# One step of a hybrid decoder layer on one core: fewer transposes in the mixer, other buffers and scales for the sample states

## The chip, the core and the metric

The kernel runs on 1 of the 8 cores of one Trainium2 chip. The time is the device time of one execution in microseconds; the table below gives the median of three runs. The core has a matrix engine (TensorE, PE in the profile; PEld is its weight load), VectorE (DVE), ScalarE (ACT), GpSimd (POOL), and a queue of transfers issued by SyncE (SP).

## The reference

One layer of width 2048 is applied to 16 learned meta tokens, 256 prompt tokens and 8 sample tokens, each sample with its own recurrent states. It is FFN, mixer, FFN, each with a residual and a layer norm.

```python
x <- LN1(alpha*x + 0.5*SwiGLU_1(x))
x <- LN2(alpha*x + Mixer(x))      # retention and HGRN2 side by side, gated, one output projection
x <- LN3(alpha*x + 0.5*SwiGLU_2(x))

# a chunk of retention (8 heads of 256), per-head decay gamma
o     = (q k^T * D) v + (q * decay) S
S_new = gamma^C S + (k * decay)^T v
# HGRN2 (16 heads of 128): the same with a forget gate f per channel and k = 1 - f
```

The prompt starts from a zero state; each sample takes one step (C = 1) from its given state, so its new state is `gamma S + k v` (retention) or `f S + k v` (HGRN2) and its output is q times that. Outputs are y for prompt and samples and the four sets of new states.

## The kernel before

Everything is held as features by tokens: 128 partitions of features, 280 columns of tokens (16 meta, 256 prompt, 8 samples). Every weight matrix is streamed once from memory in units of eight 128x128 blocks (`stream`, `raw`, three buffers). ScalarE rounds a unit to a high part (`whi`, line 187), VectorE computes the rest (`wlo`, line 188), and TensorE makes three products for each block (`dense`, line 217): high weights with the high and the low part of x, low weights with the high part.

The mixer works by u = 0 to 7: one retention head of 256 (two column blocks c = 0, 1) and two HGRN heads of 128 (h = 0, 1). `project` runs the dense projections of u (f, q_h, i_h, q_r, k_r, v_r) and the gates of u - 1. Two generators, `mix_hg(u)` and `mix_ret(u)`, do the rest of the mixer in pieces: `pump` is called after each step of a projection and lets a generator go on when the steps that it yielded are over. TensorE's instructions run in just this program order (`manual_schedule` for PE); for the other engines and SP's queue a scheduler sets the order by priority, and each engine then keeps to it.

`mix_ret(u)`, lines 978 to 1115:
- loads the first four samples' states (`load(0)`, line 988, tile `smr`; its four buffers are shared with the split keys and values `ks`, `vs`), and transposes v and k to tokens by features in blocks of 128, 128 and 24 columns (lines 998 and 1007). The last block has the last 16 prompt tokens and the 8 samples. `ks2` and `vs2` hold its high, high, low and high, low, high parts on three groups of partitions;
- writes the samples' v out to memory (`vrow`, line 720), and reads it back spread over all partitions (`spread`, line 1038, `vbr`, four samples at a time, one buffer);
- computes scores times the decay table into `scr`, in place of `dt` (line 239), and the new prompt state in two halves (line 1049), each copied to `sro` and sent out (lines 1051, 1052). `sro` has one buffer (row d9);
- `gam`, also a tile named `sro`, is set to the head's decay by POOL (line 1062). For both halves e of the samples and both c, ScalarE scales the state by `gam` (line 1067), VectorE adds k v sample by sample (line 1070), and the state goes out (line 1073); after the first half the second `spread` is issued;
- 15 or more steps later the sample products `pqr` (line 1084) multiply `qdr`, which holds each sample's q alone in its own column, with these states; the prompt's outputs follow (`por`), and the samples' rows are transposed into their columns by `sample_columns` (line 729).

`mix_hg(u)`, lines 733 to 968: doubling levels s = 1 to 64 scale K and Q by products of f in `Ts`; at levels 16 and 32 the states of the two heads are loaded (`smh`, `vbh`); then the two blocks of K and its 16 meta columns are transposed for each head (line 900), the meta part split into `km` on three groups of partitions; the sample states are scaled by f (line 906, scale from `fk`) and updated (line 907); `pq` (line 933) multiplies `qdh` with them, head h in columns h * 128 on; `sample_columns` transposes them for each head.

Of the kernel before, what the change touches and what calls it, by code (L numbers as in the profile page):

```python
# [10 lines left out]
F32 = mybir.dt.float32  # L11
# [39 lines left out]

SCORES = ((0, 0, SEQ, P), (SEQ, P - NMETA, 2 * P - P + NMETA, P), (2 * SEQ - P + NMETA, SEQ - NMETA, NMETA, LP - 2 * P))
# [75 lines left out]
def trunk(ctx: ExitStack, tc: tile.TileContext, A, O):  # L128
# [417 lines left out]
    with tc.tile_pool(name="yp", bufs=1) as yp:  # L546
# [7 lines left out]
        with tc.tile_pool(name="mp", bufs=1) as mp:  # L554
# [33 lines left out]
            qdh = tmp("qdh", (P, 2, NS * 32))  # L588
            qdr = tmp("qdr", (P, 2, NS * 32))
# [11 lines left out]
            sc2 = tmp("sc2", (P, NMETA), dt=F32R)  # L601
            for z in (km, vm, ks2, vs2, sc2):
                z = z if len(z.shape) == 2 else z.rearrange("p c f -> p (c f)")
                nc.scalar.copy(z, qdh[:, 0, : z.shape[1]])
# [106 lines left out]
            def upper_upper_lower(out, x):  # L711
# [3 lines left out]
                sub(out[64 : 64 + n], x, out[:n].bitcast(F32))  # L715
# [11 lines left out]
            def sample_columns(on, po, os):  # L727

                nc.tensor.transpose(po[:, 3 * P :], os, ident)
                nc.vector.tensor_copy(  # L730
                    on[:, SEQ:].rearrange("p (e j) -> p e j", e=2), po[:, 3 * P :].rearrange("p (j c) -> p c j", c=32)[:, 0:2, :])

            def mix_hg(u, f, k, q, v):
# [121 lines left out]
                for s in (4, 8):  # L855
                    scale_k(s)
                scale_q(8)
# [35 lines left out]
                on_h[u] = on  # L893
                kts = []
                for h in range(2):
# [6 lines left out]
                    upper_upper_lower(km[:, h, :], pt[:NMETA, 2 * P : 3 * P])  # L902

                    vb, sm = vbs[h], sms[h]
                    for b in range(NS):
                        nc.scalar.activation(sm[:, b, :], sm[:, b, :], AF.Copy, scale=fk[:, 0, h, b : b + 1])
# [30 lines left out]
                nc.scalar.copy(os, pq[:, : 2 * P])  # L937
                yield 4

                def outputs(h):  # L940
# [5 lines left out]
                    sample_columns(on[:, h, :], po, os[:, h * P : (h + 1) * P])  # L946
# [31 lines left out]
            def mix_ret(u, q, k, v):  # L978
# [15 lines left out]
                nc.sync.dma_start(dt, A["dtab"][u])  # L994
                for c in range(2):
                    pt = mx_bank("pt")
                    for b, (t0, n) in enumerate(BLOCKS):
                        nc.tensor.transpose(pt[:n, b * P : (b + 1) * P], v[:, c, t0 : t0 + n], ident)
                    nc.scalar.copy(vt[:, :, c, :], pt[:, : 2 * P].rearrange("p (b f) -> p b f", b=2))
                    nc.scalar.copy(vt2[:NB, c, :], pt[:NB, 2 * P : 3 * P])  # L1000
                    f = slice(c * P, (c + 1) * P)
                    split(vs[:, 0, :, f], vs[:, 1, :, f], vt[:, :, c, :])
                    upper_lower_upper(vs2[:, c, :], vt2[:NB, c, :])
                    yield 1
                    pt = mx_bank("pt")
                    for b, (t0, n) in enumerate(BLOCKS):
                        nc.tensor.transpose(pt[:n, b * P : (b + 1) * P], k[:, c, t0 : t0 + n], ident)
# [242 lines left out]
```

## Time and profile before

| what | us |
|---|---|
| median of 3 runs | 2607.2 (2603.62 to 2609.99) |
| the profiled execution | 2608.29 |
| its span, first to last instruction | 2606.2 |
| TensorE busy in it | 2580.9 |
| VectorE busy | 1703.7 |
| ScalarE busy | 1375.4 |
| POOL busy | 13.7 |

A row of a timeline has the start in us from the span's beginning, the length, the engine, the line of the kernel, the operation, the tile written and the tiles read, the shape, and how many instructions are merged; in brackets stands the engine's idle time before it, and what ended it. A row of waits has who waited for whom, then us in total, times, and the longest. In the grouped rows of the page, the busy us and the mean ns of one stand behind the first bar, and the engine's idle time behind the second. The ends of matmuls are modelled, since they are pipelined: the cost of one is better read from start to start.

### The profile page before, as it was taken

What the parts mean: (1) busy time and instruction counts of PE and PEld (TensorE: products, weight loads), DVE (VectorE), ACT (ScalarE), POOL (GpSimd) and SP (SyncE); (2) the same over time, 40 slices, a digit from 0 to 9 for tenths busy, and PEclk for the clock granted to TensorE, in tenths of its full rate; (3) what the DMA queues carried; (4) which work ended last, traced back from release to release, by engine and by line L of the source; (5) the groups of instructions that cost most, each with busy time, mean ns of one, the idle gap of its engine ahead of it and who ended that gap; (6) DMA issues with size and microseconds to landing.
All of it is one profiled execution on the core that took longest, in us unless ns stands there. A gap on an engine that the chain in (4) does not pass through costs nothing.

```text
span 2606.2 us, 56106 instructions
## 1 busy us (share of the span) xinstructions
PE 2580.9 (99%) x23400; PEld 2546.5 (98%) x23400; DVE 1703.7 (65%) x2859; ACT 1375.4 (53%) x2160; POOL 13.7 (1%) x62
## 2 busy tenths in 40 slices
PE   9999999999999989999999999999999999999999
PEld 9999999999999889999999999999999999999998
DVE  6444454565579777777777777776995555556555
ACT  5444444444456566666666666665564444444444
POOL 0000000000000000000000000000000000000000
PEclk9999999999999999999999999999999999999999
DMA  7555555555566675767676767676656666666664
GB/s 240 184 183 185 186 185 182 184 186 185 182 200 223 216 269 183 265 207 260 210 258 210 256 206 263 203 235 194 193 187 201 195 195 195 195 197 193 197 197 147
DMA packets 154591, 536.25 MB, mean 206 GB/s; under 512 B 17696, under 2 KB 25696, under 8 KB 154336
## 3 DMA queue, kind: packets, MB, share of 16 engines
q1 hardware_dynamic: 154048, 532.37, 63.0%
q8 instruction: 183, 3.00, 0.5%
q14 instruction: 72, 0.59, 0.1%
q10 hardware_dynamic: 288, 0.29, 0.0%
HBM read 501.99 MB, written 30.61 MB: 204 GB/s over the span
## 4 chain that ended last, share of the span: by engine, by line
PE 92%; DVE 4%; DMA 2%; ACT 1%; issue 1%; SPq 0%; POOL 0%; ACTq 0%; POOLq 0%; DVEq 0%
PE up L217 35%; PE dn L217 18%; PE pj_f L217 4%; PE pj_q_h L217 3%; PE wo L217 3%; PE pj_k_r L217 3%; PE pj_v_r L217 3%; PE pj_g_r L217 3%; PE pj_i_h L217 3%; PE pj_q_r L217 3%; PE pj_a_r L217 3%; PE pj_g_h L217 3%; PE pj_a_h L217 3%; DVE wlo L188 2%; DMA vbr<-vrd 1%; PE pqr L1084 1%
## 5 line engine op out<-in xcount | busy, mean ns | idle before, releaser
L188 DVE TENSOR_TENSOR wlo<-raw,whi 128x1024 fp32r<-128x1024 f32 (+1 forms) x869 | 1062.4, 1223 | 748.6 <-ACT whi L187 745.4
L187 ACT CAST whi<-raw 128x1024 fp32r<-128x1024 f32 (+1 forms) x870 | 905.3, 1042 | 911.4 <-PE up L217 413.1
L217 PE MATMUL up<-xh,wlo 128*128 128x280 f32 (+1 forms) x2624 | 726.0, 280 | 1.3 <-DVE wlo L188 1.3
L217 PE MATMUL up<-xh,whi 128*128 128x280 f32 (+1 forms) x2624 | 725.7, 280 | 1.0 <-ACT whi L187 1.0
L217 PE MATMUL up<-xl,whi 128*128 128x280 f32 (+1 forms) x2624 | 725.4, 279 | 0.0
L217 PEld LDWEIGHTS up<-xh,wlo 128*128 128x128 f32 x2624 | 492.5, 189 | 2.3 <-DVE wlo L188 2.3
L217 PEld LDWEIGHTS up<-xh,whi 128*128 128x128 f32 x2624 | 492.6, 189 | 1.3 <-ACT whi L187 1.2
L217 PEld LDWEIGHTS up<-xl,whi 128*128 128x128 f32 x2624 | 492.6, 189 | 0.0
L217 PE MATMUL dn<-hh,whi 128*128 128x280 f32 (+1 forms) x1376 | 384.7, 280 | 0.0
L217 PE MATMUL dn<-hh,wlo 128*128 128x280 f32 (+1 forms) x1376 | 384.3, 279 | 0.0
L217 PE MATMUL dn<-hl,whi 128*128 128x280 f32 (+1 forms) x1376 | 384.3, 279 | 0.0
L217 PEld LDWEIGHTS dn<-hh,whi 128*128 128x128 f32 x1376 | 260.1, 189 | 0.1
L217 PEld LDWEIGHTS dn<-hl,whi 128*128 128x128 f32 x1376 | 260.1, 189 | 0.1
L217 PEld LDWEIGHTS dn<-hh,wlo 128*128 128x128 f32 x1376 | 260.1, 189 | 0.0
L217 PE MATMUL pj_g_r<-xh,whi 128*128 128x264 f32 x256 | 76.8, 300 | 0.0
L217 PE MATMUL pj_g_h<-xh,whi 128*128 128x264 f32 x256 | 73.7, 288 | 0.0
L217 PE MATMUL pj_k_r<-xh,whi 128*128 128x280 f32 x256 | 73.7, 288 | 0.0
L217 PE MATMUL pj_v_r<-xh,whi 128*128 128x280 f32 x256 | 73.5, 287 | 0.0
L217 PE MATMUL pj_v_r<-xh,wlo 128*128 128x280 f32 x256 | 72.4, 283 | 0.3 <-DVE wlo L188 0.3
L217 PE MATMUL pj_k_r<-xh,wlo 128*128 128x280 f32 x256 | 72.5, 283 | 0.0
L217 PE MATMUL pj_k_r<-xl,whi 128*128 128x280 f32 x256 | 72.3, 283 | 0.0
L217 PE MATMUL pj_v_r<-xl,whi 128*128 128x280 f32 x256 | 72.3, 283 | 0.0
(393 smaller groups left out, 5235.6 us busy)
## 6 DMA issues: line engine op xcount, KB each, us to landing
raw<-in_w_up SPq DMA_DIRECT2D x343, 512.0 KB, 4.2
raw<-in_w_in SPq DMA_DIRECT2D x320, 512.0 KB, 4.5
raw<-in_w_dn SPq DMA_DIRECT2D x172, 512.0 KB, 3.4
smr<-in_sr SPq DMA_DIRECT2D x32, 512.0 KB, 4.7
out_srs<-smr SPq DMA_DIRECT2D x32, 512.0 KB, 4.7
raw<-in_w_out SPq DMA_DIRECT2D x32, 512.0 KB, 3.5
smh<-in_sg SPq DMA_DIRECT2D x16, 512.0 KB, 4.7
vbr<-vrd SPq DMA_DIRECT2D x16, 512.0 KB, 4.1
```

What stands on the lines that cost most here:

```text
L187: nc.scalar.copy(hi[:, j:jn, :], raw[:, j:jn, :])
L188: nc.vector.tensor_tensor(out=lo[:, j0:j1, :], in0=raw[:, j0:j1, :], in1=hi[:, j0:j1, :].bitcast(F32), op=ALU.subtract)
L217: nc.tensor.matmul(o, w, t, start=start, stop=stop)
L1084: nc.tensor.matmul(pq[32 * j : 32 * j + 32, :256], qdr[:, c, 32 * b : 32 * b + 32], sms[2 * e + c][:, j, :], start=e + c == 0, stop=e + c ...
```

## The change

- Retention, transposes: only the two blocks of 128 of v and k are transposed for each c. POOL copies the 24 last columns of k and v for both c into `tails` (four groups of 32 columns), which is transposed once, at c = 0. `dec2` is the decay for the last block on two groups of partitions.
- HGRN, transposes: POOL copies K's 16 meta columns of both heads into `meta`, transposed once, with head 0.
- HGRN, samples: `qdh` now puts the q of head h and half e in column 2h + e, so the products of both heads add up in the same 128 columns of `pq`; `osh` has half the width, and one transpose serves both heads. `qdr` gets the same layout, with the same columns as before.
- HGRN, scales: the scaling of the states reads `fs`, a POOL copy of the samples' f that takes the buffer of `T64`, a product of the last doubling level.
- Retention, states: `sro` has two buffers (d9 and a new row, d16). The first half's scale is `gam`, a POOL instruction on `scr` that is clamped to the decay; only the second half's is a memset of an `sro` tile. `vbr` has two samples to a transfer, on two buffers; the first two are issued together, and each further one when the four updates that read an older one are issued. Both scalings of a half come ahead of its updates, and both outgoing transfers behind them.

```diff
-                "sro": "d9",
+                "sro": ["d9", "d16"],
-            qdh = tmp("qdh", (P, 2, NS * 32))
+            qdh = tmp("qdh", (P, 4, ALONE))
+            qdh_at = [qdh.rearrange("p a c -> p (a c)")[:, 256 * h :] for h in range(2)]
+            qdr_at = [qdr.rearrange("p a c -> p (a c)")[:, 2 * ALONE * c :] for c in range(2)]
...
             def alone(qd, q):
-                for e in range(2):
-                    nc.vector.tensor_copy(qd[:, :, 128 * e + e : 128 * e + 128 : 32], q[:, :, SEQ + 4 * e : SEQ + 4 * e + 4])
+                nc.vector.tensor_copy(
+                    qd[:, :, : 128 : 32].rearrange("p (c e) j -> p c e j", e=2),
+                    q[:, :, SEQ:].rearrange("p c (e j) -> p c e j", e=2))
...
@@ mix_hg @@
+                nc.gpsimd.tensor_copy(meta[:, :, :NMETA], K[:, :, :NMETA])
...
+                fs = tmp("fs", (P, 2, NS), tag="T64")
+                nc.gpsimd.tensor_copy(fs, fk[:, 0])
...
-                    for b, (t0, n) in enumerate(((NMETA, P), (NMETA + P, P), (0, NMETA))):
-                        nc.tensor.transpose(pt[:n, b * P : (b + 1) * P], K[:, h, t0 : t0 + n], ident)
+                    for b in range(2):
+                        t0 = NMETA + b * P
+                        nc.tensor.transpose(pt[:, b * P : (b + 1) * P], K[:, h, t0 : t0 + P], ident)
+                    x = pt[:64, 2 * P : 3 * P]
+                    if h == 0:
+                        nc.tensor.transpose(x, meta.rearrange("p h t -> p (h t)"), ident)
+                        for i in range(2):
+                            upper_upper_lower(km[:, i, :], x[32 * i : 32 * i + NMETA], 32 * i)
...
-                        nc.scalar.activation(sm[:, b, :], sm[:, b, :], AF.Copy, scale=fk[:, 0, h, b : b + 1])
+                        nc.scalar.activation(sm[:, b, :], sm[:, b, :], AF.Copy, scale=fs[:, h, b : b + 1])
...
-                            pq[j : j + 32, h * P : (h + 1) * P], qdh[:, h, 32 * b : 32 * b + 32], sms[h][:, b, :],
-                            start=b < 4, stop=b >= 4, tile_position=(0, j))
-                os = tmp("osh", (P, 2 * P))
+                            pq[j : j + 32, :P], qdh_at[h][:, 32 * b : 32 * b + 32], sms[h][:, b, :],
+                            start=h == 0 and b < 4, stop=h == 1 and b >= 4, tile_position=(0, j))
+                os = tmp("osh", (P, P))
...
-                    sample_columns(on[:, h, :], po, os[:, h * P : (h + 1) * P])
+                    if h == 0:
+                        sample_columns(on, po, os)
...
@@ mix_ret @@
+                for i, x in enumerate((k, v)):
+                    nc.gpsimd.tensor_copy(tails[:, 2 * i : 2 * i + 2, :NB], x[:, :, 2 * P :])
                 for c in range(2):
                     pt = mx_bank("pt")
-                    for b, (t0, n) in enumerate(BLOCKS):
-                        nc.tensor.transpose(pt[:n, b * P : (b + 1) * P], v[:, c, t0 : t0 + n], ident)
+                    for b in range(2):
+                        nc.tensor.transpose(pt[:, b * P : (b + 1) * P], v[:, c, b * P : (b + 1) * P], ident)
...
-                    for b, (t0, n) in enumerate(BLOCKS):
-                        nc.tensor.transpose(pt[:n, b * P : (b + 1) * P], k[:, c, t0 : t0 + n], ident)
+                    for b in range(2):
+                        nc.tensor.transpose(pt[:, b * P : (b + 1) * P], k[:, c, b * P : (b + 1) * P], ident)
+                    if c == 0:
+                        nc.tensor.transpose(pt[:, 2 * P : 3 * P], tails.rearrange("p i t -> p (i t)"), ident)
...
+                gams = [tmp("gam", (P, 1))]
+                nc.gpsimd.tensor_scalar(
+                    out=gams[0], in0=scr[:, 0:1], scalar1=GAMMA[u], scalar2=GAMMA[u], op0=ALU.min, op1=ALU.max)
...
-                def spread(e):
-                    vbs.append(tmp("vbr", (P, 4, 256)))
-                    nc.sync.dma_start(vbs[e], vrow[4 * e : 4 * e + 4, :].partition_broadcast(P))
+                def spread(i):
+                    if i < 4:
+                        vbs.append(tmp("vbr", (P, 2, 256), bufs=2))
+                        nc.sync.dma_start(vbs[i], vrow[2 * i : 2 * i + 2, :].partition_broadcast(P))
 
                 spread(0)
+                spread(1)
...
-                gam = tmp("sro", (P, 1))
-                nc.gpsimd.memset(gam, GAMMA[u])
+                gams.append(tmp("sro", (P, 1)))
+                nc.gpsimd.memset(gams[1], GAMMA[u])
                 for e in range(2):
-                    vb = vbs[e]
+                    ss = sms[2 * e : 2 * e + 2]
+                    for sm in ss:
+                        nc.scalar.activation(sm, sm, AF.Copy, scale=gams[e])
+                    for i in (2 * e, 2 * e + 1):
+                        for c in range(2):
+                            for b in (2 * i, 2 * i + 1):
+                                x, t = ss[c][:, b - 4 * e, :], LP + b
+                                nc.vector.scalar_tensor_tensor(
+                                    out=x, in0=vbs[i][:, b - 2 * i, :], scalar=k[:, c, t : t + 1], in1=x, op0=ALU.mult, op1=ALU.add)
+                        spread(i + 2)
                     for c in range(2):
-                        sm = sms[2 * e + c]
-                        nc.scalar.activation(sm, sm, AF.Copy, scale=gam)
-                        for j in range(4):
-                            t = LP + 4 * e + j
-                            nc.vector.scalar_tensor_tensor(
-                                out=sm[:, j, :], in0=vb[:, j, :], scalar=k[:, c, t : t + 1], in1=sm[:, j, :],
-                                op0=ALU.mult, op1=ALU.add)
-                        nc.sync.dma_start(O["srs"][u, c, :, 4 * e : 4 * e + 4, :], sm)
-                    if e == 0:
-                        spread(1)
+                        nc.sync.dma_start(O["srs"][u, c, :, 4 * e : 4 * e + 4, :], ss[c])
```

More of the change, by code (lines that the diff above doesn't have):

```diff
@@ L601, in trunk @@
             sc2 = tmp("sc2", (P, NMETA), dt=F32R)
+            tails = tmp("tails", (P, 4, 32))
+            meta = tmp("meta", (P, 2, 32))
+            nc.gpsimd.memset(tails, 0.0)
+            nc.gpsimd.memset(meta, 0.0)
+            dec2 = tmp("dec2", (P, HR))
+            for i in range(2):
+                nc.scalar.copy(dec2[32 * i : 32 * i + T - 2 * P], dec[: T - 2 * P, 2, :])
             for z in (km, vm, ks2, vs2, sc2):
                 z = z if len(z.shape) == 2 else z.rearrange("p c f -> p (c f)")
-                nc.scalar.copy(z, qdh[:, 0, : z.shape[1]])
+                nc.scalar.copy(z, qdh_at[0][:, : z.shape[1]])
             threads = []
@@ L933, in mix_hg @@
                         nc.tensor.matmul(
[L934 to L937 removed]
+                            pq[j : j + 32, :P], qdh_at[h][:, 32 * b : 32 * b + 32], sms[h][:, b, :],
+                            start=h == 0 and b < 4, stop=h == 1 and b >= 4, tile_position=(0, j))
+                os = tmp("osh", (P, P))
+                nc.scalar.copy(os, pq[:, :P])
                 yield 4
@@ L1013, in mix_ret @@
                         nc.vector.scalar_tensor_tensor(
-                            out=(ks[:, 1, b, f] if b < 2 else ks2[third[2], c, :]), in0=x, scalar=g,
-                            in1=his[0].bitcast(F32), op0=ALU.mult, op1=ALU.subtract)
+                            out=lo, in0=x, scalar=g, in1=his[i].bitcast(F32), op0=ALU.mult, op1=ALU.subtract)
+                    if c == 0:
+                        for i in range(2):
+                            r = 64 + 32 * i
+                            nc.scalar.copy(vt2[:NB, i, :], pt[r : r + NB, 2 * P : 3 * P])
+                        upper_lower_upper(vs2.rearrange("p c f -> p (c f)"), vt2.rearrange("p c f -> p (c f)")[:NB])
                     yield 2
@@ L1084, in mix_ret @@
                             nc.tensor.matmul(
-                                pq[32 * j : 32 * j + 32, :256], qdr[:, c, 32 * b : 32 * b + 32],
+                                pq[32 * j : 32 * j + 32, :256], qdr_at[c][:, 32 * b : 32 * b + 32],
                                 sms[2 * e + c][:, j, :], start=e + c == 0, stop=e + c == 2, tile_position=(0, 32 * j))
```

26 lines of the change are left out of this document (15 added, 11 removed), and 2 rows, old and new, of the table rows.

## The prediction

> **What bounds the kernel now.** The page comes first. It says that TensorE is busy for nearly the whole span, so a gain has to come from work that TensorE no longer does or from time in which it stands.
>
> ```profile
> span 2606.2 us, 56106 instructions
> PE 2580.9 (99%) x23400; PEld 2546.5 (98%) x23400; DVE 1703.7 (65%) x2859; ACT 1375.4 (53%) x2160; POOL 13.7 (1%) x62
> ```
>
> A busy share hides slow matmuls, so the next view is the waits: first TensorE's, then those of the engine it waits for.
>
> ```profile
> PE pqr L1084 <- DVE smr L1070: 9.9, 3, 5.2
> ACT smr L1067 <- POOL sro L1062: 9.3, 6, 5.2
> DVE smr L1070 <- DMA vbr<-vrd: 18.4, 8, 4.1
> ```
>
> One wait dominates TensorE's: the sample products of the retention heads (pqr, line 1084) wait 9.9 us for VectorE's state update (smr, line 1070). That update waits in turn for the broadcast rows (vbr) and for ScalarE's scaling, which waits for POOL's one-column memset (sro, line 1062).
>
> Behind the first product the others can crawl without counting as idle. So I asked for the busy time of line 1084 alone, one stretch for each head u = 0 to 7. Columns: stretch, its length, PE busy (records), granted clock, DMA share, GB/s.
>
> ```profile
> 850.00:870.00 20.00, 4.91 (x32) 0.83 0.94 292
> 960.00:980.00 20.00, 5.49 (x32) 0.83 0.88 314
> 1085.00:1100.00 15.00, 2.71 (x32) 1.00 0.83 296
> 1215.00:1225.00 10.00, 2.90 (x32) 1.00 0.78 265
> 1345.00:1355.00 10.00, 2.51 (x32) 1.00 0.79 279
> 1475.00:1485.00 10.00, 3.31 (x32) 1.00 0.75 258
> 1604.00:1614.00 10.00, 1.94 (x32) 1.00 0.77 258
> 1732.00:1742.00 10.00, 1.94 (x32) 1.00 0.81 290
> ```
>
> The same 32 records take 1.94 us when nothing is late (u = 6, 7). The eight sum to 25.7 us, 8 x 1.94 is 15.5, so 10.2 us are slow products. With the 9.9 us of idle time the stall costs **20.1 us**: u = 0 has 4.91 + 4.17 - 1.94 = 7.1, u = 1 has 5.49 + 5.7 (9.9 less 4.2) - 1.94 = 9.3, and u = 2 to 5 have 3.7 together. The two idle stretches are these:
>
> ```profile
> 862.42 3.83 PE L1084 MATMUL pqr<-smr,qdr 128*32 128x256 f32 x16 [4.17 <-DVE smr L1070]
> 972.16 1.06 PE L1084 MATMUL pqr<-smr,qdr 128*32 128x256 f32 x2 [5.24 <-DVE smr L1070]
> ```
>
> Last, the order of time on the other engines ahead of the first of them (u = 0), and two rows of u = 1.
>
> ```profile
> 831.28 0.56 DVE L239 TENSOR_TENSOR dtab<-psc,dtab 128x400 f32<-128x400 f32 x1
> 834.39 0.34 SPq L1052 DMA_DIRECT2D out_srp<-sro  x1
> 837.06 0.37 ACT L1051 COPY sro<-psr 128x256 f32<-128x256 f32 x1 [2.69 <-DMA out_srp<-sro]
> 837.89 0.86 SPq L988 DMA_DIRECT2D smr<-in_sr  x2
> 841.82 0.10 POOL L1062 MEMSET sro<- 128x1 f32 x1 [40.53 <-DMA out_srp<-sro]
> 846.49 2.19 ACT L1067 ACTIVATE smr<-smr,sro 128x1024 f32<-128x1024 f32 x2
> 848.18 0.48 DVE L1070 SCALAR_TENSOR_TENSOR smr<-vbr,k_r,smr 128x256 f32<-128x256 f32 x1
> 854.68 0.43 SPq L1038 DMA_DIRECT2D vbr<-vrd  x1
> 861.88 3.25 DVE L1070 SCALAR_TENSOR_TENSOR smr<-vbr,k_r,smr 128x256 f32<-128x256 f32 x8 [2.97 <-DMA vbr<-vrd]
> ...
> 938.18 0.56 DVE L239 TENSOR_TENSOR dtab<-psc,dtab 128x400 f32<-128x400 f32 x1
> 952.67 0.10 POOL L1062 MEMSET sro<- 128x1 f32 x1 [79.48 <-DMA out_srp<-sro]
> ```
>
> The memset shares the buffer of the two outgoing prompt states, so it waits until the second has left (841.82). Only then does the first half of the samples start; its last update ends at 848.66, and the second broadcast reuses the one vbr buffer, behind it in SP's order (854.68). Its data come 7.2 us after the issue, and the last eight updates end at 865.1, where TensorE wanted them from about 858. For u = 1 the memset is 14 us behind the scores (938.7).
>
> **The change, part by part.**
>
> *Transposes.* For each head pair u, the third transpose goes from both v blocks and from one k block (the other becomes the joint one); one meta transpose serves both K blocks; and one sample transpose serves both HGRN heads. That is 3 + 1 + 1 = 5 fewer, 40 in all. The price of one is read from start to start of the same matmul around a group:
>
> ```profile
> 1254.30 10.80 PE pj_q_h L217 x96
> ...
> 1278.18 0.28 PE L217 MATMUL pj_q_r<-xl,whi 128*128 128x264 f32 x1
> 1278.40 0.38 PE L834 MATMUL pt<-ident,v 128*128 128x128 f32 x2
> 1278.73 0.28 PE L217 MATMUL pj_q_r<-xl,whi 128*128 128x264 f32 x1
> ...
> 1314.87 0.28 PE L217 MATMUL pj_g_r<-xl,whi 128*128 128x264 f32 x1
> 1315.43 0.49 PE L998 MATMUL pt<-ident,v 128*128 128x128 f32 x3
> 1315.88 0.28 PE L217 MATMUL pj_g_r<-xl,whi 128*128 128x264 f32 x1
> ```
>
> A wide matmul takes 10.80 / 96 = 0.1125 us. The first pair of starts is 0.55 us apart with three of them: two transposes cost 0.21. The second is 1.01 apart with six: three transposes cost 0.335, so the third, of 24 columns, costs 0.12, no less than a full one. With 0.335 / 3 = 0.112, 40 give **4.5 us**. Bounds: 3.6 if the eight sample transposes, which stand behind matmuls of another kind, cost nothing; 4.8 at 0.12.
>
> [...]
>
> *The stall.* Three edits bear on it. The outgoing state gets two buffers, so ScalarE's 2.69 us wait at 837.06 goes. The decay scale of the first half comes from a small POOL instruction on the scores, so it is there one POOL instruction after 831.84; the dearest such row is 0.97 us (below), so about 833 instead of 841.9. And vbr comes in quarters on two buffers, the third issued once four updates, not eight, are done. The weight casts that share these engines last as long as the page says:
>
> ```profile
> L188 DVE TENSOR_TENSOR wlo<-raw,whi 128x1024 fp32r<-128x1024 f32 (+1 forms) x869 | 1062.4, 1223 | 748.6 <-ACT whi L187 745.4
> L187 ACT CAST whi<-raw 128x1024 fp32r<-128x1024 f32 (+1 forms) x870 | 905.3, 1042 | 911.4 <-PE up L217 413.1
> ```
>
> Taking two scalings (2.19) with a cast (1.04) between as 4 us on ScalarE, and four updates (a half of 3.25) with one subtraction (1.22) as 3 us on VectorE, the third quarter is issued at about 840 and the fourth 2 to 3 us later. At the slow 7.2 us landing they are there by 847 and 850. The second half's states are issued at 837.89 or earlier and its scale needs only the first outgoing state, gone at 837.06. Eight updates with two casts between take 6 us, the last behind the fourth quarter: they end near 853, before 858. For u = 1 the same steps start from 938.7 instead of 952.67 and end about 961, before the 966.9 at which the second half is wanted (972.16 less the idle 5.24). u = 2 to 5 lack at most 1.4 us each and gain far more. Bounds of this part: all 20.1 us, or nothing if the landing rather than the start decides. I take 19, since the spacing of several steps is mine, not a row's.
>
> *Added work.* SP issues four vbr transfers for two, of the same bytes; each waits in SP's order for its updates, with weight loads behind it. POOL gets two copies for the ragged ends (tails), one of K (meta), one of the sample decays (fs), and the scale. TensorE waits for tails one projection step after v. The slack is read from the heads where v comes late:
>
> ```profile
> 1536.36 0.97 POOL L737 COPY ends<-v 128x32 f32<-128x32 f32 x1 [73.17 <-ACT v L658]
> 1573.32 0.40 ACT L675 COPY v<-pj_v_r 128x280 f32<-128x280 f32 x1
> 1574.90 0.49 PE L1007 MATMUL pt<-ident,k_r 128*128 128x128 f32 x3
> ```
>
> v is there at 1573.72, and the transpose stands third in a group that starts at 1574.90, so at about 1575.1. A copy like that of ends, 0.97 us, leaves 0.4 us. Bounds: nothing, or half a microsecond more than the slack for each head, 4 us. I take 1. The meta copy has several levels of pumping to hide in, and fs is due only at the products of line 933, tens of projection steps on; both at nothing while they run ahead. ScalarE and VectorE lose four short instructions per head, both off the path.
>
> [...]
>
> *Sum.* The profiled execution took 2608.3 us, 2.1 around its span of 2606.2, and lies 1.1 above the median of 2607.2. From it: 2608.3 - 4.5 - 19 + 1 = 2585.8; I forecast **2586 us**.
>
> **The rivals.**
>
> *Half of the stall stays.* In the stretches of u = 0 and 1 the DMA share is 0.94 and 0.88. If the queues are full without the idle time in which they now catch up, broadcasts and states land later than I put them, and weight loads behind a waiting broadcast too. Half of the 16.4 us of these two would stay: 2586 + 8 = 2594. Against it: the bytes are the same and the first half's start moves by 9 to 14 us.
>
> *The change does not do what it says.* If ScalarE and VectorE keep the old order of the updates, or the scale is late again, only the transposes count: 2608.3 - 4.5 + 1 = 2605. Against it: the scale no longer depends on the transfer at all.
>
> *Slower: the fs copy bunches the HGRN state updates.* All 16 scalings and 16 updates of a pair now stand behind the last doubling level; before, the first head's ran earlier.
>
> ```profile
> 850.39 1.28 ACT L906 ACTIVATE smh<-smh,fk 128x128 f32<-128x128 f32 x4
> 946.73 2.19 DVE L907 SCALAR_TENSOR_TENSOR smh<-vbh,fk,smh 128x128 f32<-128x128 f32 x8
> ```
>
> That is 16 x 0.32 = 5.1 us of ScalarE and 16 x 0.27 = 4.4 of VectorE. If they run as one block ahead of the weight casts and nothing covers them, TensorE waits 4.5 to 5 us in each of eight units: 2585.8 + 38 = 2624. It decides from (22.5 + 7.8) / 8 = 3.8 us per unit. Against it: a unit of weights lasts 24 x 0.1125 = 2.7 us and three are buffered, some 8 us; and the block of eight at 946.73 let no matmul of its neighbourhood wait.
>
> **How the numbers follow.** The forecast gets 0.64, half of the stall 0.18, transposes alone 0.11, slower 0.04; 0.03 is left for a schedule that moves work in ways the old trace cannot show. The range of 8 in 10 runs from 2579 (every stalled microsecond back, no added cost, and some of the weight waits beside the stall gone too) to 2602 (three quarters of the stall left). A measurement of this kernel tells about 0.3%, 7.8 us, from no change, so faster means below 2599.4. All of the forecast, most of the half-stall case and a little of the rest lie there: 0.83; within 0.3%: 0.12; slower: 0.05.
>
> **What would show it.** Right: line 1084 busy near 1.94 us in every head and no wait of TensorE on smr above a microsecond; 40 transposes fewer; the second half's updates ending before the products. The scale step is wrong if line 1067 still waits on POOL; the quarters are if the third lands after the products begin; tails cost if TensorE shows waits on POOL. Weight waits (whi, wlo) growing past their present few microseconds would speak for the last rival. The forecast fails if two or more of the old stalls return in u = 0 and 1.

## The result

| | median us | runs | ratio to before, 95% interval |
|---|---|---|---|
| before | 2604.35 | 5 (2603.62 to 2609.99) | |
| after | 2616.98 | 5 (2615.26 to 2619.80) | 1.0045 [1.0034, 1.0056] |

The change makes the kernel 0.45% slower, where 2586 us was forecast; the prediction gave slower a chance of 0.05. The kernel before has two more runs here than in the table ahead of the prediction, and its median is 2.85 us lower. The stall that the prediction was about is gone all the same. The views of the changed kernel, in the same order as before: the page, then the waits (of TensorE first), then the sample products alone (now line 1120), one stretch for each head (its length, busy time and records of PE and of its weight loads, granted clock, DMA share, GB/s).

```profile
span 2615.1 us, 56028 instructions
PE 2576.5 (99%) x23360; PEld 2549.7 (97%) x23360; DVE 1703.5 (65%) x2827; ACT 1378.4 (53%) x2146; POOL 39.6 (2%) x104
```

```profile
PE psr L1085 <- DVE vs L255: 20.4, 7, 4.9
PE ptk L917 <- DVE K L240: 4.0, 1, 4.0
PE psc L1056 <- ACT kth L923: 2.2, 1, 2.2
```

```profile
850.00:870.00 20.00, 1.94 (x32) 0.97 (x32) 1.00 0.95 314
...
1730.00:1765.00 35.00, 1.94 (x32) 0.96 (x32) 1.00 0.74 254
sum 210.00, PE 15.50 PEld 7.69; mean PE 1.94 PEld 0.96
```

Forty TensorE instructions fewer (23400 to 23360), 1.94 us of sample products in every head, and no wait on smr: both savings are there. But TensorE, which was busy 4.4 us less, stands in new places. The largest is psr (line 1085), the product that makes the new prompt state: 20.4 us for VectorE's write of vs, as much as the old stall cost. The next view follows this wait in one head, u = 4, across ScalarE, VectorE, TensorE and SP; the first row is TensorE's transpose of the joint ends, into the bank of PSUM (`pt`) that holds k's full blocks too.

```profile
1314.58 0.27 PE L1031 MATMUL pt<-ident,tails 128*128 128x128 f32 x1
1315.55 0.36 ACT L1039 ACTIVATE ks<-pt,dec 128x128 fp32r<-128x128 f32 x1
1318.00 0.60 DVE L1040 SCALAR_TENSOR_TENSOR ks<-pt,dec,ks 128x128 fp32r<-128x128 f32 x2
1318.88 1.12 ACT L1039 ACTIVATE ks<-pt,dec 24x128 fp32r<-24x128 f32 x3
1320.58 0.72 DVE L1040 SCALAR_TENSOR_TENSOR ks<-pt,dec,ks 24x128 fp32r<-24x128 f32 x2
1320.95 0.73 ACT L1039 ACTIVATE ks<-pt,dec 24x128 fp32r<-24x128 f32 x2 [0.96 <-DVE ks L1040]
1322.27 1.15 ACT L1102 ACTIVATE smr<-smr,gam 128x1024 f32<-128x1024 f32 x1
1323.14 0.83 PE L1085 MATMUL psr<-vs,ks 128*128 128x256 f32 x6
1323.33 1.03 ACT L188 CAST whi<-raw 128x1024 fp32r<-128x1024 f32 x1
1324.26 0.53 ACT L1045 COPY vt<-pt 24x128 f32<-24x128 f32 x2
1324.82 0.29 SPq L730 DMA_DIRECT2D vrd<-vt  x1
1326.17 0.41 DVE L255 TENSOR_TENSOR vs<-vt,vs 24x256 fp32r<-24x256 f32 x1
1326.73 0.35 PE L1085 MATMUL psr<-vs,ks 128*128 128x256 f32 x1 [2.75 <-DVE vs L255]
```

The joint transpose is done at 1314.85, and v's end leaves the bank at 1324.26, 9.4 us later: behind k's full blocks and k's two ends, whose ScalarE and VectorE steps on the one bank take turns (ScalarE stands 0.96 us for VectorE's), then behind the state scaling, which is now ready early (`gam`), and a weight cast. The seventh psr product needs it and waits 2.75 us. In the kernel before, the same head had v's end beside v's own blocks, in a bank without k's work:

```profile
1318.91 0.25 ACT L1000 COPY vt<-pt 24x128 f32<-24x128 f32 x1
1319.40 0.32 SPq L720 DMA_DIRECT2D vrd<-vt  x1
...
1325.43 0.94 PE L1049 MATMUL psr<-vs,ks 128*128 128x256 f32 x7
```

There v's end left PSUM at 1318.91, 6.5 us ahead of the first psr product, and psr had no wait; now it does so at 1324.26, 5.4 us later and 1.1 us behind the first six products (1323.14). The waits of all heads are 4.95 and 1.66 us at u = 0 and 1 and five of 2.75 us at u = 2 to 6.

For the account of TensorE's time I summed its timeline from start to start between the first projection of u = 0 and the first output product, with the idle time put to the tile that waited. It has the experiments' columns too; they are named below.

| us | before | after | e3 | e8 | e9 | e14 |
|---|---|---|---|---|---|---|
| sample products pqr | 35.6 | 15.5 | 71.4 | 27.7 | 15.5 | 15.5 |
| prompt states psr | 13.7 | 36.7 | 23.8 | 17.1 | 13.4 | 12.6 |
| scores psc | 10.1 | 13.7 | 12.1 | 10.1 | 10.1 | 10.1 |
| transposes | 17.8 | 19.4 | 13.4 | 17.8 | 17.8 | 17.0 |
| of it without idle time | 17.3 | 13.8 | 13.4 | 17.3 | 17.3 | 13.5 |
| projections | 910.9 | 914.7 | 911.9 | 914.0 | 910.3 | 909.6 |
| the whole stretch | 1056.2 | 1067.0 | 1099.0 | 1058.9 | 1037.2 | 1034.6 |

### The profile page after: what moved, and what is told of

Its sections match the earlier page's. It is cut to its first block, busy times and chain, and to the rows that moved or that the text cites. A ratio compares the mean times of both kernels' runs of the same rounds, so it can differ in the third digit from the quotient of the medians.

```text
span 2615.1 us, 56028 instructions
## 1 busy us (share of the span) xinstructions
PE 2576.5 (99%) x23360; PEld 2549.7 (97%) x23360; DVE 1703.5 (65%) x2827; ACT 1378.4 (53%) x2146; POOL 39.6 (2%) x104
## 4 chain that ended last, share of the span: by engine, by line
PE 90%; DVE 4%; ACT 3%; DMA 2%; issue 1%; SPq 0%; POOL 0%; ACTq 0%; DVEq 0%; POOLq 0%
PE up L218 36%; PE dn L218 18%; PE pj_v_r L218 4%; PE wo L218 3%; PE pj_k_r L218 3%; PE pj_g_h L218 3%; PE pj_a_h L218 3%; PE pj_q_r L218 3%; PE pj_f L218 3%; PE pj_q_h L218 3%; PE pj_i_h L218 3%; PE pj_g_r L218 2%; PE pj_a_r L218 2%; DVE wlo L189 2%; ACT whi L188 1%
## 5 line engine op out<-in xcount | busy, mean ns | idle before, releaser
L218 PE MATMUL pj_g_r<-xh,wlo 128*128 128x264 f32 x256 | 71.3, 279 | 1.2 <-DVE wlo L189 1.2
```

What stands on the lines that cost most here:

```text
L218: nc.tensor.matmul(o, w, t, start=start, stop=stop)
```

## The experiments

Ratios are to runs of the kernel before beside them.

| | what it is | median us | ratio, 95% interval |
|---|---|---|---|
| e1 | after, v's end first | 2594.02 | 0.9951 [0.9936, 0.9965] |
| e2 | after, both halves scaled late | 2600.40 | 0.9978 [0.9968, 0.9987] |
| e3 | joint transposes alone | 2652.20 | 1.0179 [1.0159, 1.0200] |
| e4 | state edits alone | 2596.50 | 0.9961 [0.9948, 0.9974] |
| e5 | e3, v's end first | 2611.78 | 1.0026 [1.0012, 1.0040] |
| e6 | e1 without fs | 2597.14 | 0.9968 [0.9957, 0.9979] |
| e7 | after, v's end before k's end | 2590.31 | 0.9947 [0.9932, 0.9962] |
| e8 | before, early scale alone | 2607.87 | 1.0013 [1.0004, 1.0022] |
| e9 | before, quarters alone | 2587.85 | 0.9934 [0.9918, 0.9951] |
| e10 | e4 without fs | 2597.43 | 0.9973 [0.9962, 0.9983] |
| e11 | joint transposes, v's end between, quarters | 2594.43 | 0.9959 [0.9946, 0.9971] |
| e12 | joint transposes, v's end first, quarters | 2589.13 | 0.9938 [0.9924, 0.9951] |
| e13 | e12, kt copy first | 2585.98 | 0.9929 [0.9915, 0.9942] |
| e14 | e7, kt copy first | 2585.45 | 0.9923 [0.9910, 0.9935] |

### First round: the late end, and the two halves of the change

The first theory was that v's end was late by the order within the joint bank; the rival, that the early scaling took ScalarE ahead of it. e1 moves the five instructions of v's end ahead of k's work on the same bank.

```diff
+                    if c == 0:
+                        for i in range(2):
+                            r = 64 + 32 * i
+                            nc.scalar.copy(vt2[:NB, i, :], pt[r : r + NB, 2 * P : 3 * P])
+                        upper_lower_upper(vs2.rearrange("p c f -> p (c f)"), vt2.rearrange("p c f -> p (c f)")[:NB])
                     todo = [(pt[:, b * P : (b + 1) * P], dec[:, b, u : u + 1], [ks[:, 0, b, f]], 0, ks[:, 1, b, f]) for b in range(2)]
...
-                    if c == 0:
-                        for i in range(2):
-                            r = 64 + 32 * i
-                            nc.scalar.copy(vt2[:NB, i, :], pt[r : r + NB, 2 * P : 3 * P])
-                        upper_lower_upper(vs2.rearrange("p c f -> p (c f)"), vt2.rearrange("p c f -> p (c f)")[:NB])
                     yield 2
```

> Change with one block moved: the ragged end of v leaves PSUM and is split into vs2 ahead of k's work on the same transpose. Theory A (v's end is late because it stands behind k's end in the chain of ScalarE and VectorE steps on one PSUM tile): TensorE's wait of psr for vs (20.4 us in 7) is gone, the busy time of psr is back near 1.9 us a head, and the time is 2617 - 23 (psr) - 5 (matmuls at the lower clock behind the waits) = about 2589. Theory B (the state scaling, ready early now, takes ScalarE ahead of it): one scaling and a cast, 2.2 us, still stand before vs, the wait shrinks by no more than half, 2605 or more.

e2 keeps v's end last, and scales both halves from the one late memset.

```diff
-                gams = [tmp("gam", (P, 1))]
-                nc.gpsimd.tensor_scalar(
-                    out=gams[0], in0=scr[:, 0:1], scalar1=GAMMA[u], scalar2=GAMMA[u], op0=ALU.min, op1=ALU.max)
...
-                gams.append(tmp("sro", (P, 1)))
+                gams = [tmp("sro", (P, 1))] * 2
                 nc.gpsimd.memset(gams[1], GAMMA[u])
```

> Change with both halves of the samples scaled by one memset behind the outgoing state, as before; transposes, two sro buffers and vbr in quarters stay. Theory A: the wait of psr for vs stays at 1.5 us or more a head (some 12 us), since only one scaling of 1.15 us goes from in front of it; time 2605 to 2615. Theory B: the wait is gone; part of the pqr stall is back instead; time 2590 to 2600.

e1 took the psr wait away wholly, and 2594.02 is 23 us under the changed kernel. e2 left 2.5 us of it, 2.1 of that at u = 0 and 1, and has the sample products at 17.5 us, 2 more than the changed kernel. So in the five middle heads both are needed for the wait: the order within the bank puts v's end where the early scaling can get in ahead of it. In the first two heads the late end is enough by itself, as e3 shows below. e1 is 5 us above its theory A and still 8 us above the forecast.

e3 and e4 split the change in two: e3 is the changed kernel with the states, scales and `fs` of before, e4 the kernel before with the changed ones.

> The transposes of the change alone; the state updates, buffers, broadcasts and scales are those of before. Theory A: psr waits for vs, 10 to 20 us, pqr stalls by about 20 us as before: 2604 - 4.5 + 10 to 25 = 2610 to 2625. Theory B: no wait of psr: 2604 - 4.5 = 2600.

> The state part of the change alone (two sro buffers, scale on the scores, vbr in quarters, fs); all transposes are those of before. Theory A: pqr takes 1.94 us in each head, 15.5 in all, no wait of psr for vs above 1 us in total: 2604 - 20 = 2584. Theory B: psr waits for vs here too, 10 us or more: 2594 or more.

```profile
PE pqr L1113 <- DVE smr L1099: 32.4, 8, 4.6
PE psr L1078 <- DVE vs L255: 9.9, 2, 6.8
```

These are waits of TensorE in e3: the transposes alone cost 46 us, twice what theory A allowed at most. The psr wait is at u = 0 and 1 only (6.8 and 3.1 us), though nothing is scaled early. The broadcast of the samples' v starts from v's end as well (`vrd`, then `vbr`; at 1319.40 before and 1324.82 after in the rows above), so a late end makes the state updates late in all eight heads. The state edits alone gain 10 us, not the 20 of theory A, although pqr is at 15.5; the third round finds a part of what is missing. With v's end first the two together gain 12. This is why the change as a whole lost only 12.6: its state edits make up for a broadcast that its transposes delay (pqr 15.5 us in the one, 71.4 in the other).

### Second round: is it all the late end, and which edit removes the stall

e5 is e3 with e1's edit; e6 is e1 without the copy of the sample decays (`scale=fk[...]` again); e7 puts v's end behind k's full blocks but ahead of k's end; e8 is the kernel before with two `sro` buffers and the early scale alone.

The edit of e7 against the changed kernel, and that of e8 against the kernel before:

```diff
-                    if c == 0:
-                        for i in range(2):
-                            r = third[i]
-                            todo.append((pt[r, 2 * P : 3 * P], dec2[r, u : u + 1], [ks2[q, i, :] for q in third[:2]], i, ks2[third[2], i, :]))
                     for x, g, his, i, lo in todo:
...
                         upper_lower_upper(vs2.rearrange("p c f -> p (c f)"), vt2.rearrange("p c f -> p (c f)")[:NB])
+                    todo = []
+                    if c == 0:
+                        for i in range(2):
+                            r = third[i]
+                            todo.append((pt[r, 2 * P : 3 * P], dec2[r, u : u + 1], [ks2[q, i, :] for q in third[:2]], i, ks2[third[2], i, :]))
+                    for x, g, his, i, lo in todo:
...
```

```diff
+                gams = [tmp("gam", (P, 1))]
+                nc.gpsimd.tensor_scalar(
+                    out=gams[0], in0=scr[:, 0:1], scalar1=GAMMA[u], scalar2=GAMMA[u], op0=ALU.min, op1=ALU.max)
                 vbs = []
...
-                gam = tmp("sro", (P, 1))
-                nc.gpsimd.memset(gam, GAMMA[u])
+                gams.append(tmp("sro", (P, 1)))
+                nc.gpsimd.memset(gams[1], GAMMA[u])
...
-                        nc.scalar.activation(sm, sm, AF.Copy, scale=gam)
+                        nc.scalar.activation(sm, sm, AF.Copy, scale=gams[e])
```

> The joint transposes alone, with the states of before, but v's ragged end taken out of PSUM ahead of k's work. Theory A (the late end of v, and the broadcast of its sample rows behind it, are all of what the joint transposes cost): the 46 us that they cost alone go. The psr products lose their wait on vs, the pqr products wait about as in the kernel before (5 to 15 us in all), and the time is the kernel before's less the 4.5 us of the transposes, 2602 us (2598 to 2606). Theory B (the joint transposes also delay the states in another way, by k's ragged end or by the ends' copies on POOL): pqr still waits 20 us or more, and the time stays above 2615 us.

> The changed kernel with v's ragged end first, and without the copy of the sample decays (the HGRN scalings read the decay tile itself, as before). Theory A (the copy neither costs nor brings anything): the time stays that of the version with the copy, 2594 us within 2, with the same waits of ptk and pl of 2 to 4 us. Theory B (the copy bunches the sample updates of the HGRN heads, and the waits of ptk and pl that are left come of that): these waits go, and the time falls by 4 to 8 us, to 2586 to 2590 us.

> The changed kernel with v's ragged end behind k's two full blocks of the first channel block, but ahead of k's ragged end; before it, it came last. Theory A (what made v's end late is the alternation of ScalarE and VectorE over k's ragged end, and the state scaling that got in ahead of it): the psr wait on vs goes (below 2 us in all), 2594 us within 3, as with v's end first. Theory B (any work of k ahead of it is too much): a wait of 1 us or more stays in each of the five middle heads, and the time is 2600 us or more.

> The kernel before with two of the state edits alone: two buffers for the outgoing states and the scale of the first half of the samples taken from the scores. The broadcast rows stay in halves on one buffer, and there is no copy of the sample decays. Theory A (the late start of the first half was what made pqr wait, as the prediction put it): pqr's idle time falls from 9.9 to below 2 us, and the time to 2597 us within 3, as with all state edits. Theory B (the second half's broadcast, whose one buffer comes free late, decides): pqr still waits 5 us or more, and the time is 2601 us or more.

e5 brings 40 of e3's 46 us back (2652.20 to 2611.78), and psr's wait on vs is gone; but it lands at 1.0026, 6 us over the kernel before instead of 4.5 under it. The late end was the most of it, not all. e6 gives no sign that the `fs` copy costs anything: without it the time is 3 us higher, and the waits of ptk and pl stay at 2.9 and 2.4 us. e7 gives 2590.31 us; its interval overlaps that of e1, so which of the two places is better is not shown. Its rows of the same head (u = 4):

```profile
1301.80 0.53 ACT L1041 COPY vt<-pt 24x128 f32<-24x128 f32 x2
1303.38 0.41 DVE L255 TENSOR_TENSOR vs<-vt,vs 24x256 fp32r<-24x256 f32 x1
1305.55 1.15 ACT L1108 ACTIVATE smr<-smr,gam 128x1024 f32<-128x1024 f32 x1
1305.95 0.94 PE L1091 MATMUL psr<-vs,ks 128*128 128x256 f32 x7
```

The scaling is just as early there, but behind v's end instead of ahead of it, and psr does not wait.

e8 was the surprise. The early scale alone takes the idle time of pqr (9.9 to 0.9 us) but not its slow products, and the time does not fall at all: the 7.9 us that pqr loses come back, and more, as waits of psr for ks (3.8 us) and of the doubling products pl for Q (3.7), and as 3.1 more on the projections. The stretches of line 1087 in e8, for the first and the sixth head (columns as above):

```profile
840.00:870.00 30.00, 3.65 (x32) 1.43 (x32) 0.89 0.88 294
...
1460.00:1496.00 36.00, 3.41 (x32) 1.46 (x32) 1.00 0.81 279
```

They take 3.4 to 3.7 us instead of 1.94: the products have begun, but crawl behind the second half's broadcast, as two rows of the fifth head show.

```profile
1343.36 3.25 DVE L1073 SCALAR_TENSOR_TENSOR smr<-vbr,k_r,smr 128x256 f32<-128x256 f32 x8 [1.89 <-DMA vbr<-vrd]
1344.16 3.13 PE L1087 MATMUL pqr<-smr,qdr 128*32 128x256 f32 x29
```

### Third round: the quarters

e9 is the complement of e8: the kernel before with `vbr` in quarters on two buffers, and the updates in the order that goes with them; one `sro` buffer and one late memset stay. e10 is e4 without `fs`. The lines of e9 beside the kernel before (the loop over the updates is the change's):

```diff
-                def spread(e):
-                    vbs.append(tmp("vbr", (P, 4, 256)))
-                    nc.sync.dma_start(vbs[e], vrow[4 * e : 4 * e + 4, :].partition_broadcast(P))
+                def spread(i):
+                    if i < 4:
+                        vbs.append(tmp("vbr", (P, 2, 256), bufs=2))
+                        nc.sync.dma_start(vbs[i], vrow[2 * i : 2 * i + 2, :].partition_broadcast(P))
...
                 gam = tmp("sro", (P, 1))
                 nc.gpsimd.memset(gam, GAMMA[u])
...
+                        nc.scalar.activation(sm, sm, AF.Copy, scale=gam)
```

> The kernel before with the broadcast rows in quarters on two buffers alone; the outgoing states keep their one buffer, and both halves wait for the memset behind the second of them. Theory A (start and quarters each remove a part of the stall, and only together all of it): pqr loses its slow products in the middle heads but keeps most of the idle time of the first two, 5 to 12 us in all above its 15.5, and the time is 2600 us within 3. Theory B (the quarters are what matters, the start costs nothing): pqr falls to 16 us or less, and the time to 2597 us or below.

> The kernel before with the outgoing states' two buffers, the scale from the scores and the quarters, but without the copy of the sample decays. Theory A (the copy has no part in it): pqr at 15.5 us without idle time, and 2596.5 us within 2, as with the copy. Theory B (the copy is what keeps the HGRN updates out of the state updates' way): pqr keeps 3 us or more above 15.5, and the time is 2600 us or more.

e9 bears out its theory B and goes further: 2587.85 us, 0.9934, with pqr at 15.5; e10 its theory A. The timeline of e9 at u = 0 (POOL's memset, SP's issue of the fourth quarter, VectorE's last four updates), and behind it VectorE's last updates in e10 and the last two of these rows in the changed kernel:

```profile
839.16 0.10 POOL L1064 MEMSET sro<- 128x1 f32 x1 [39.33 <-DMA out_srp<-sro]
846.06 0.38 SPq L1039 DMA_DIRECT2D vbr<-vrd  x1
852.28 1.67 DVE L1073 SCALAR_TENSOR_TENSOR smr<-vbr,k_r,smr 128x256 f32<-128x256 f32 x4
```

```profile
850.58 1.27 DVE L1076 SCALAR_TENSOR_TENSOR smr<-vbr,k_r,smr 128x256 f32<-128x256 f32 x3
```

```profile
845.67 0.38 SPq L1073 DMA_DIRECT2D vbr<-vrd  x1
852.63 1.67 DVE L1107 SCALAR_TENSOR_TENSOR smr<-vbr,k_r,smr 128x256 f32<-128x256 f32 x4
```

The memset of e9 still waits for the outgoing state, until 839.16, and its last update ends at 853.95, 2.65 us ahead of the first sample product (856.60). In e10, with the early scale, the last update ends at 851.85, 2.1 us sooner, and no product waited for it in either; in the changed kernel, whose broadcast is issued at 833.09 (in e10 at 827.68), it ends at 854.30. The early start gained nothing where it counts. By e10 against e9 it cost 9.6 us (its two `sro` buffers with it), and the next rows show one place of that, at u = 1. They are VectorE's state updates and its last doubling product of K, and TensorE's transposes of K behind it; first e10, then e9.

```profile
951.75 1.67 DVE L1076 SCALAR_TENSOR_TENSOR smr<-vbr,k_r,smr 128x256 f32<-128x256 f32 x4 [0.50 <-DMA vbr<-vrd]
954.81 1.67 DVE L1076 SCALAR_TENSOR_TENSOR smr<-vbr,k_r,smr 128x256 f32<-128x256 f32 x4
958.22 0.43 DVE L239 TENSOR_TENSOR K<-K,T 128x256 f32<-128x256 f32 x1
958.79 0.88 PE L900 MATMUL ptk<-ident,K 128*128 128x128 f32 x3 [3.12 <-DVE K L239]
```

```profile
951.23 0.43 DVE L239 TENSOR_TENSOR K<-K,T 128x256 f32<-128x256 f32 x1
951.71 0.55 PE L900 MATMUL ptk<-ident,K 128*128 128x128 f32 x3
953.72 1.68 DVE L1073 SCALAR_TENSOR_TENSOR smr<-vbr,k_r,smr 128x256 f32<-128x256 f32 x4
```

With the early scale the second half's updates stand ahead of K in VectorE's queue; K comes at 958.22 and TensorE waits 3.12 us. In e9 K goes first. The changed kernel has the same order as e10 here, and a wait of 4.0 us (the `ptk` row of its waits).

### Fourth and fifth round: the joint transposes again

e11 and e12 join the transposes to e9's quarters, with v's end between k's blocks and k's end, or first.

> The joint transposes with v's ragged end ahead of k's ragged end, and of the state edits the quarters alone: one buffer for the outgoing states, one memset behind them, no copy of the sample decays. Theory A (the quarters take the stall away, the transposes save their 4 us, and the two do not disturb each other once v's end is early and nothing is scaled early): 2583.5 us within 2, pqr at 15.5 us, psr without a wait. Theory B (the joint transposes take their saving back wherever the sample rows come later than before): a wait of pqr, psr or psc of 3 us or more stays, and the time is 2587 us or more.

> The same, with v's ragged end first of all in the shared bank. Theory A: as with v's end in the middle, 2583.5 us within 2. Theory B (v's end ahead of k's full blocks delays the products that need k): a wait of psr on ks of 2 us or more, and 2587 us or more.

Neither reached 2583.5: e11 has 2594.43, e12 2589.13. The 4 us of transposes went back, and e11 is 6.6 us slower than e9 besides. Among the waits that e9 does not have in the same places are psr on ks (2.2 and 1.1) and psc on kth (3.4 and 2.5). The last one was in every kernel so far with the joint transposes (0.9 to 3.5 us) and in none without, and a line of the change stands behind it: the copy of K's two full blocks (`kt`) now comes after the splits of the joint meta columns (four casts on ScalarE, two subtractions on VectorE); it came ahead of the splits of its own head. Rows of the last head, kernel before and after (km and kth on ScalarE, psc on TensorE):

```profile
1705.94 0.37 ACT L901 COPY kth<-ptk 128x256 f32<-128x256 f32 x1
1706.21 0.25 ACT L713 CAST km<-ptk 16x128 fp32r<-16x128 f32 x1
...
1708.76 1.52 PE L1025 MATMUL psc<-q_r,k_r 128*128 128x256 f32 x8
```

```profile
1713.68 0.24 ACT L723 CAST km<-ptk 16x128 fp32r<-16x128 f32 x1
...
1717.56 0.37 ACT L923 COPY kth<-ptk 128x256 f32<-128x256 f32 x1
1717.98 3.00 PE L1056 MATMUL psc<-q_r,k_r 128*128 128x256 f32 x8 [2.23 <-ACT kth L923]
```

The bank comes free 3.9 us after the first split instead of ahead of it; psc waits 2.23 us and then takes twice its time. e13 and e14 put the copy first, in e12 and in e7.

```diff
                     if h == 0:
                         nc.tensor.transpose(x, meta.rearrange("p h t -> p (h t)"), ident)
+                    nc.scalar.copy(kt, pt[:, : 2 * P].rearrange("p (b f) -> p b f", b=2))
+                    if h == 0:
                         for i in range(2):
                             upper_upper_lower(km[:, i, :], x[32 * i : 32 * i + NMETA], 32 * i)
-                    nc.scalar.copy(kt, pt[:, : 2 * P].rearrange("p (b f) -> p b f", b=2))
```

> The version with v's end first and the quarters alone, and in the joint transpose of K the copy of the two full blocks (kt) ahead of the four splits of the meta columns, where the kernel before had it for its own bank. Theory A (the same fault as with v's end: a step that everything waits for was put behind the rest of a joint bank; the retention scores of the last head wait 2.5 us for that copy and run at half speed behind it): the wait of psc on kth goes, psc falls from 11.5 us to 10.1 in all, and the time falls by 3 to 5 us, to 2585 us within 2. Theory B (the bank is free late in any order): the wait stays above 1.5 us, and the time is 2588 us or more.

> The changed kernel whole (early scale, quarters, joint transposes, copy of the sample decays), with v's end ahead of k's ragged end and the copy of kt ahead of the splits of the meta columns. Theory A: the wait of 3.5 us of psc goes, and the time falls from 2590.3 to 2586 us within 2, what the prediction gave the change. Theory B: the wait stays or goes elsewhere, and the time is 2589 us or more.

Both came out as theory A had it: e13 at 2585.98 us, e14 at 2585.45 (0.9923), and psc has no wait on kth in either (10.4 and 10.1 us). The intervals of e13 and e12 overlap, and so, by a little, do those of e14 and e7: the wait shows the effect more clearly than the time. e14 is the change as it was made, whole, with two groups of instructions in another order, and it has the time that was forecast for it.

## Why the prediction was wrong

**The step that failed** is in "Added work": "ScalarE and VectorE lose four short instructions per head, both off the path." The page has VectorE with 32 instructions fewer, four for each head, and ScalarE with 14 fewer in all, so the count was about right. But the transpose that was joined also joined what was read from it, and v's end moved from v's banks to the end of k's queue of steps: 5.4 us later at u = 4. I priced the wait for the copy into `tails`, ahead of the transpose, and never asked who reads the bank behind it, in what order, and who waits for the last reader: psr's seventh product, and the broadcast of the samples. The size: moving v's five instructions to the front (e1) is worth 23 us, moving them less far and `kt` too (e14) 31.5 us. Scaling early had a part in it: with v's end still last, going back to the late scale (e2) is worth 16.6 us.

The same step was missed a second time with K: `kt` behind the meta splits costs e7 2590.3 - 2585.5 = 4.8 us. The prediction spoke only of POOL's copy into `meta`, for which TensorE shows no wait.

The turns that ScalarE and VectorE take on the joint bank from 1318.00 on are measured (0.96 us of ScalarE's time at u = 4, 7.7 us in eight waits of the whole run); VectorE's steps there also read what ScalarE's wrote, and no run here took the order away. In the joint bank k's end lies on partitions 0 to 55 and v's end on 64 to 119, and v's end stood behind k's all the same: at u = 0 of e2 the copies of v's end, at 828.72, wait 0.51 us for VectorE's last step on k's end. So joining transposes in one bank joined their readers into one queue here, and e1 and e7 moved v's end forward in it.

**The transposes: right on TensorE.** From first projection to first projection, the head without a stall before (u = 6) took 128.26 us, and in e14 it takes 127.70: 0.56 us for five transposes, 5 x 0.112 as predicted. Four of the five are short ones, so these cost as much as full ones here. In the whole time the saving is not clear of noise: e13 and e14 lie 2 us under e9, which has none of the joint transposes, and the intervals overlap.

**The stall: the size right, the cause wrong.** Predicted 19 of 20.1 us; all 20.1 went, and the updates of u = 0 end at 854.30 where "near 853" was worked out. That second agreement is luck: the early scale was held up by the late broadcast, and in e14, without the late end, they end at 849.66. But three edits were put down for it, the start first. e8 and e9 show that the start alone takes 7.9 (35.6 to 27.7) and brings no time, and the quarters alone take all. The prediction had this as its other bound ("if the landing rather than the start decides"), and read from it only a loss: that the landing could be improved alone was there, since the second `vbr` waited for the first's last reader. Being early was taken to be free; e10 against e9 puts its price at 9.6 us with the transposes of before. One place of it is shown, K behind the updates on VectorE (3.1 us); that the rest comes of queue places too is argued, not shown. With both orders mended no such price shows (e14 with it 2585.45, e13 without it 2585.98, which also differ in `fs` and in the place of v's end).

**Tails on POOL:** 1 us was put in; TensorE has no row of a wait for `tails` in the changed kernel. **fs:** the slower rival, 38 us by bunched HGRN updates, did not come: with and without the copy the times are 2594.0 and 2597.1 (e1, e6), 2596.5 and 2597.4 (e4, e10). The sign that the prediction named for failure, the old stalls coming back, did not show either; what it lacked was a rival in which the joint bank delays its last reader.

**Open:** e11 is 5 us slower than e12, and e5 6 us over the kernel before, by waits of 1 to 3 us on ks, kth and weight parts in different heads. Which of them comes with which order I can't tell from these runs. So it stays open, too, whether v's end is better first (e12 against e11) or between (e7 against e1).

## What to carry over

When transposes or products are joined in one bank, write down every reader of that bank in order and what waits for each; the reader on the critical path goes first, whatever its place in the source was (v's end moved forward: 23 us in e1). Work made ready early goes into a queue ahead of something (the updates ahead of K in e10: a wait of 3.12 us): look at what stands behind it there, not only at its own end. And split a change that has parts: the quarters alone gain 0.66% [0.49, 0.82], which the whole as it was made turned into a loss.

## Not expected of the hardware

The same wait was followed by slow matmuls in some heads and not in others. The first five stretches hold the 2.75 us waits of psr in the changed kernel, which end at 1062.04, 1194.39, 1326.73, 1457.42 and 1589.76 (TensorE busy, granted clock, DMA share, GB/s); the last two the psc wait.

```profile
1062.00:1066.00 4.00, 3.96 (x21) 0.59 0.83 281
1194.00:1199.00 5.00, 4.61 (x27) 0.68 0.78 211
1326.00:1331.00 5.00, 4.27 (x38) 1.00 0.85 276
1457.00:1462.00 5.00, 4.58 (x26) 0.66 0.81 239
1589.00:1594.00 5.00, 4.24 (x38) 1.00 0.81 247
...
1715.00:1718.00 3.00, 0.77 (x8) 1.00 0.77 307
1718.00:1721.00 3.00, 3.00 (x10) 0.51 0.55 175
```

Three of the five lose the clock behind the wait, with 11 or 12 matmuls fewer where the stretch is 5 us long; at 1326.73 and 1589.76 nothing is lost. From start to start, the three have about 16 matmuls at 0.21 to 0.22 us instead of 0.11, a slow stretch of 3.4 us that costs some 1.6 us each time. A wait of 2.2 us was enough at 1717.98 to run eight products in 3.00 us that take 1.52. So waits of 2.2 to 2.75 us cost the clock in some heads here, and 2.75 us cost nothing in two of five; what decides it no run here shows. In this kernel a wait of that size is to be priced with nothing or some 1.5 us of slow products behind it.
